# One decoder layer on one core: the attention's query and key stacks loaded with one DMA each, ahead of other loads

## The chip, the core and the metric

The kernel runs on one core of one Trainium2 chip. The core has five engines that each work through an instruction list of their own, in order: TensorE (PE in the profile, with its weight loads as PEld), VectorE (DVE), ScalarE (ACT), GpSimd (POOL) and SyncE (SP). Data moves between the memory of the chip and the on-chip memory of 128 partitions by DMA; here SP starts most transfers, ACT and POOL some, and the core's 16 DMA engines carry all of them. An instruction starts when the semaphores that it waits for have come and the one before it on its engine has left. The metric is the device time of one execution in microseconds (us), lower is better.

## The reference

The reference is one layer of a decoder over 1024 tokens of width 1024, in float32. Two kinds of attention run side by side and are merged by gates; a gated MLP with a causal convolution follows.

```python
xn = rmsnorm(x, norm_mix_w[l])
proj = xn @ w_in[l]
da_q, da_k, da_v, sw_q, sw_k, sw_v, g_da, g_sw = split_cols(proj)
y_da = diff_attention(da_q, da_k, da_v, lam, lam_init, subln_w[l])
y_sw = sliding_window_attention(sw_q, sw_k, sw_v, sinks[l])
merged = jax.nn.sigmoid(g_da) * (y_da @ w_br_da[l]) + jax.nn.sigmoid(g_sw) * (y_sw @ w_br_sw[l])
x = x + merged @ w_mix_out[l]
xn = rmsnorm(x, norm_ffn_w[l])
x = x + conv_ffn(xn, w_up[l], conv_w[l], conv_b[l], w_down[l])
```

The change touches the first kind, `diff_attention`, and the loads of the second. It has 4 heads with two query and key components of 64 each:

```python
s = jnp.einsum('bqhcd,bshcd->bhcqs', q_blk, k) * scale
logits = s - slopes[:, None, None, None] * dist.astype(jnp.float32)
logits = jnp.where(dist >= 0, logits, NEG_INF)
p = jax.nn.softmax(logits, axis=-1)
a = p[:, :, 0] - lam * p[:, :, 1]
return jnp.einsum('bhqs,bshe->bqhe', a.astype(v.dtype), v)
```

## The kernel before

**Two parts of a number.** TensorE multiplies numbers of reduced precision here, so the kernel keeps a value as a high part and a low part (what is left after rounding) and adds products of the parts. Queries and keys are stored that way in a buffer `qd` in the chip's memory: `qd[m, 0]` holds the high parts of the 128 channels of row block m, `qd[m, 1]` the low parts, each as 128 x 1024 (channel, token).

**The projection** makes query, key, value and gate channels in pairs of 128-row blocks; each pair is put together from seven partial products. The results stand in tiles `us`. `keep` stores queries and keys as high and low part (`qd<-hi` L628, `qd<-us` L629); gate blocks of these pairs are stored to `gd` at L589. The last of the pairs, blocks 21 and 22, are gates.

**The attention** starts at about 235 us. Its order is written out by hand in the table `STEPS`, whose words are run one after the other; a helper `in_order` keeps the engines to that order. The words that matter here are:
- `lqu_c` and `lku_c`: load of a query stack, and of two key stacks, for unit u and component c. A stack is a tile `u` of 128 partitions x 1024 tokens with 64 channels in its upper and 64 in its lower half. The query stack has the high parts in one half and the low parts in the other; the two key stacks repeat the high, and the low, parts in both halves. Product over 128 partitions of such stacks then sums high and low terms in one pass. There are 11 places for `u` tiles, handed out in turn (`turns`, `done`), and 36 stacks in all.
- `lvu`: load of a value block of unit u, into a tile `f` (`v32`, L796); `Xvu_0` and `Xvu_4`: its transposes on TensorE (L776).
- `Su_i_c`: scores of query block i (`sc<-u,u`, L811 for units 0 to 3; L953 for the sliding window, units 4 and 5), which read one query stack and two key stacks. `R` adds `bias` on VectorE (L817), `E` is the exponential on ScalarE (L822), `J` joins the two components.
- `Gm_h_p`: four products of gate blocks 23 to 33 (L295 to L297), set between the attention's steps, so that TensorE has work while VectorE and ScalarE are at the softmax. `wl`, `wc`, `wo` load their weights (`raw`, L264) and split them.

**Loads of a stack.** Each stack takes two DMAs of 64 partitions from SP, one a half:

```python
for part, to in enumerate((a, b)):
    self.nc.sync.dma_start(s[to].bitcast(F32), self.qd[m, part, a])
```

All of them, the weights' loads and the stores above stand in SP's one list. The bias table (128 x 1280) is loaded at L656 as the attention's tiles are set up. Where a tile lies is decided when it is first asked for, so that a stack can lie where a tile of the projection lay, and its load then waits until that tile has been read.

Of the kernel before, what the change touches and what calls it, by code (L numbers as in the profile page):

```python
# [17 lines left out]
P = 128  # L18
D = 1024
T = 1024  # L20
# [5 lines left out]
EPS = 1e-6  # L26
RAW = 3
GATE = 23
LATE = (21, 22, *range(26, 34))
HP, HPB, HR = 7, 13, 11  # L30
STORE = (1, 6)
# [13 lines left out]

STEPS = (
    """
    G23_0_0 G23_1_0 G23_0_1 G23_0_2 G23_0_3 Z0_0_0 G23_1_1 G23_1_2 g23_0 wl24 d23_0 wl25 wl26 G23_1_3 lv0 lv1 wc24 wo24 Xv0_0 wc25 wo25 g23_1 G24_0_0
    Z0_0_1 Z0_1_0 G24_0_1 Xv0_4 lq0_0 lq0_1 lk0_0 Hv0_4 Hv0_0 Wv0_0 Wv0_4 G24_0_2 G24_0_3 S0_0_0 G24_1_0 lk0_1 S0_1_0 g24_0 R0_0_0 S0_0_1 E0_0_0 R0_0_1
    E0_0_1 R0_1_0 E0_1_0 G24_1_1 S0_1_1 S0_2_0 J0_0 G24_1_2 lq1_0 R0_1_1 E0_1_1 X0_0_0 H0_0_0 S0_2_1 R0_2_0 S0_3_0 E0_2_0 J0_1 X0_1_0 wl27 H0_1_0 R0_2_1  # L50
    R0_3_0 lq1_1 G25_0_0 Z0_1_1 Z0_2_0 S0_3_1 W0_0_0 W0_1_0 A0_0 R0_3_1 Z0_2_1 lk1_0 E0_3_0 E0_2_1 J0_2 S0_4_0 G25_0_1 E0_3_1 K0_0 X0_2_0 J0_3 R0_4_0
    S0_4_1 d23_1 R0_4_1 H0_2_0 E0_4_0 X0_3_0 wl28 S0_5_0 G25_0_2 lv2 S0_5_1 W0_2_0 R0_5_0 S0_6_0 H0_3_0 W0_3_0 A0_1 E0_4_1 R0_5_1 E0_5_1 K0_1 G24_1_3 J0_4
    R0_6_0 Z0_3_0 X0_4_0 E0_5_0 X0_4_4 J0_5 H0_4_0 W0_4_0 S0_6_1 S0_7_0 G25_0_3 R0_6_1 H0_4_4 X0_5_0 W0_4_4 X0_5_4 d24_0 E0_6_0 H0_5_0 H0_5_4 S0_7_1 g24_1
    G25_1_0 lk1_1 R0_7_0 S1_0_0 W0_5_0 W0_5_4 A0_2 E0_6_1 E0_7_0 R0_7_1 sq0_0 E0_7_1 S1_0_1 J0_6 R1_0_0 X0_6_0 d24_1 G25_1_1 lq2_0 lq2_1 K0_2 X0_6_4 J0_7
    lk2_0 Z0_3_1 Z1_0_0 G25_1_2 H0_6_0 W0_6_0 X0_7_0 wc26 wo26 wl29 G25_1_3 H0_6_4 W0_6_4 X0_7_4 g25_0 H0_7_0 W0_7_0 E1_0_0 wc27 H0_7_4 S1_1_0 R1_0_1
    R1_1_0 E1_0_1 S1_1_1 R1_1_1 W0_7_4 A0_3 E1_1_1 cs0_0 E1_1_0 S1_2_0 S1_2_1 K0_3 sq0_1 wo27 Xv1_0 J1_0 cs0_1 R1_2_0 E1_2_0 ms0 G26_0_0 Xv1_4 J1_1 d25_0
    wl30 lv3 R1_2_1 Hv1_0 g25_1 Wv1_0 Hv1_4 Wv1_4 G26_0_1 E1_2_1 J1_2 d25_1 S1_3_0 S1_3_1 X1_0_0 Z1_0_1 R1_3_0 H1_0_0 X1_1_0 W1_0_0 H1_1_0 W1_1_0 G26_0_2
    S1_4_0 A1_0 pw0 sp0_0 R1_3_1 S1_4_1 R1_4_0 S1_5_0 ny0_0 X1_2_0 Z1_1_0 E1_3_0 E1_3_1 K1_0 sp0_1 J1_3 H1_2_0 R1_4_1 W1_2_0 G26_0_3 X1_3_0 H1_3_0 R1_5_0
    E1_4_0 ny0_1 E1_4_1 S1_5_1 Z1_1_1 W1_3_0 Z1_2_0 G26_1_0 R1_5_1 E1_5_1 A1_1 K1_1 S1_6_0 sq1_0 J1_4 R1_6_0 E1_5_0 E1_6_0 X1_4_0 Z1_2_1 X1_4_4 J1_5
    Z1_3_0 G26_1_1 H1_4_4 S1_6_1 S1_7_0 R1_6_1 H1_4_0 W1_4_0 G26_1_2 W1_4_4 E1_6_1 R1_7_0 X1_5_0 H1_5_0 W1_5_0 X1_5_4 H1_5_4 S1_7_1 S2_0_0 lk2_1 lq3_0  # L60
    R1_7_1 E1_7_0 E1_7_1 G26_1_3 wc28 W1_5_4 A1_2 K1_2 Z1_3_1 Z2_0_0 J1_6 R2_0_0 lq3_1 lk3_0 g26_0 X1_6_0 H1_6_0 S2_0_1 S2_1_0 X1_6_4 J1_7 H1_6_4 d26_0
    E2_0_0 G27_0_0 W1_6_0 W1_6_4 R2_0_1 E2_0_1 R2_1_0 X1_7_0 H1_7_0 W1_7_0 J2_0 X1_7_4 sy0 H1_7_4 W1_7_4 g26_1 G27_0_1 S2_1_1 S2_2_0 d26_1 A1_3 cs1_0
    Z2_1_1 R2_1_1 E2_1_0 R2_2_0 E2_1_1 E2_2_0 wo28 wl31 J2_1 S2_2_1 R2_2_1 K1_3 Xv2_0 S2_3_0 sq1_1 cs1_1 Hv2_0 Wv2_0 ms1 pw1 E2_2_1 J2_2 R2_3_0 G27_0_2
    Xv2_4 Hv2_4 S2_3_1 X2_0_0 E2_3_0 G27_1_0 Wv2_4 X2_1_0 H2_0_0 H2_1_0 Z2_0_1 Z2_1_0 S2_4_0 R2_3_1 E2_3_1 S2_4_1 W2_0_0 W2_1_0 A2_0 Z2_2_0 Z2_2_1 sp1_0
    R2_4_0 S2_5_0 Z2_3_0 J2_3 K2_0 ny1_0 E2_4_0 X2_2_0 H2_2_0 R2_4_1 E2_4_1 G27_0_3 lv4 sp1_1 W2_2_0 X2_3_0 H2_3_0 R2_5_0 E2_5_0 S2_5_1 S2_6_0 ny1_1
    G27_1_1 W2_3_0 R2_5_1 J2_4 R2_6_0 A2_1 E2_5_1 S2_6_1 K2_1 X2_4_0 E2_6_0 X2_4_4 J2_5 R2_6_1 H2_4_4 H2_4_0 W2_4_0 sq2_0 S2_7_0 G27_1_2 E2_6_1 X2_5_0
    H2_5_0 W2_4_4 X2_5_4 R2_7_0 H2_5_4 E2_7_0 S2_7_1 S3_0_0 W2_5_0 R2_7_1 E2_7_1 g27_0 G27_1_3 W2_5_4 A2_2 K2_2 lk3_1 lq4_0 lq4_1 J2_6 X2_6_0 R3_0_0
    S3_0_1 S3_1_0 lq4_2 X2_6_4 J2_7 Z2_3_1 Z3_0_0 H2_6_0 R3_0_1 G28_0_0 S3_1_1 R3_1_0 S3_2_0 d27_0 W2_6_0 H2_6_4 W2_6_4 E3_0_0 E3_0_1 J3_0 X2_7_0 X2_7_4
# [44 lines left out]
class Trunk:  # L113
# [281 lines left out]
    def project(self):  # L395
# [6 lines left out]
        with ExitStack() as ctx:  # L402
# [171 lines left out]
            for j, ms in enumerate(self.pairs):  # L574
                w = self.next_w()
                for _ in range(4):
                    with tc.issue_after(self.sync), tc.issue_after(self.sum):
                        next(sums, None)
                pp = {}
                for name, a, b in (prods[i] for i in ((0, 1, 4, 2, 3, 5, 6) if j == 0 else (0, 1, 2, 5, 3, 4, 6))):  # L580
                    pp[name] = bank()
                    self.product(pp[name], w[a], b)
                us = [self.tl(tp, [P, T], "us", bufs=3) for _ in range(2)]
                self.recombine(pp, us, tp, 0)
                for m, u in zip(ms, us):
                    if m < 21:
                        nc.gpsimd.tensor_tensor(u, u, self.rstd, ALU.mult)
                    if self.kind[m] == "g":
                        nc.sync.dma_start(self.gd[m - 18], u)  # L589
                    else:  # L590
                        self.keep(m, u, (tp, "hi"))
                if j == 5:
                    for n, t in enumerate(self.sum_pair((self.w_up[0], self.w_up[NF]))[2:]):
                        nc.sync.dma_start(self.su[n], t)
# [37 lines left out]
    def attention(self, gctx):  # L632
        nc, tc = self.nc, self.tc
        with ExitStack() as ctx:
            e = ctx.enter_context
            self.ap = e(tc.tile_pool(name="ap", bufs=1, side="right", reuse_waits="tile"))
            self.fpool = e(tc.tile_pool(name="fyp", bufs=1, side="right", reuse_waits="tile"))
            ap = self.ap

            lt = self.tl(self.gpool, [P, 64], "g0", bufs=1)  # L640
            ls = self.st.tile([P, 4], F32, name="ls")
            for c in range(2):
                a = C_LAM + 128 * c
                nc.vector.tensor_tensor(lt, self.vecs[:, a:a + 64], self.vecs[:, a + 64:a + 128], ALU.mult)
                nc.vector.tensor_reduce(ls[:, c:c + 1], lt, axis=mybir.AxisListType.X, op=ALU.add)
            nc.scalar.activation(ls[:, 2:4], ls[:, 0:2], AF.Exp)
            self.neglam = self.cp.tile([P, 1], F32, name="neglam")
            nc.vector.tensor_tensor(self.neglam, ls[:, 3:4], ls[:, 2:3], ALU.subtract)
            nc.vector.tensor_scalar(self.neglam, self.neglam, LAM_INIT, None, ALU.subtract)
            self.nsink = self.cp.tile([P, 8], F32, name="nsink")  # L650
            nc.vector.tensor_scalar(self.nsink, self.vecs[:, C_SINK:C_SINK + 8], -1.0, None, ALU.mult)
            self.subw = self.cp.tile([P, 1], F32, name="subw")
            nc.vector.tensor_scalar(self.subw, self.vecs[:, C_SUB:C_SUB + 1], 1.0 - LAM_INIT, None, ALU.mult)

            self.bias = ap.tile([P, T + 256], F32, name="bias")
            nc.sync.dma_start(self.bias, self.bias_d)  # L656

            self.step, self.free, self.held = {}, {}, {}
            self.actx = ctx.pop_all()
            for u in range(4):  # L660
                self.da_steps(u)
            for u in range(2):
                self.sw_steps(u)
            self.gate_steps()
            self.last_steps(gctx)
            self.last = {e: None for e in (self.hi.ins.engine, self.lo.ins.engine, self.pow.ins.engine, self.pe.engine)}
            with self.in_order(self.last):
                self.steps(0)
            assert not self.step, list(self.step)
# [23 lines left out]
    def gate_steps(self):  # L693
# [34 lines left out]
        for m in range(GATE, 34):  # L728
# [5 lines left out]
            for name, f in (("wl", load), ("wc", cast), ("wo", low)):  # L734
                at(f"{name}{m + 1}", f, m + 1)

    def stack_steps(self, u, qs, k, cs):

        v = {"q": [], "k": []}

        def q(m, c):
            a, b = slice(c * 64, c * 64 + 64), slice(64 - c * 64, 128 - c * 64)
            s = self.turns(self.ap, [P, T], "u", 11, F32R, uses=NB)
            for part, to in enumerate((a, b)):
                self.nc.sync.dma_start(s[to].bitcast(F32), self.qd[m, part, a])
            v["q"].append(s)

        def keys(c):
            r = []
            for part in range(2):  # L750
                t = self.turns(self.ap, [P, T], "u", 11, F32R, uses=NB)
                for to in range(2):
                    self.nc.sync.dma_start(t[64 * to:64 * to + 64].bitcast(F32), self.qd[k, part, c * 64:c * 64 + 64])
                r.append(t)
            v["k"].append(r)

# [32 lines left out]
    def da_steps(self, u):  # L789
# [3 lines left out]

        def v32():
            v["f"] = self.turns(self.fpool, [P, T], "f", 2, uses=2)
            nc.sync.dma_start(v["f"], self.qd[8 + u, 0])  # L796

        at(f"lv{u}", v32)
        value = lambda p: once(v, ("v", p), lambda: self.turns(ap, [P, NB, P], "v", 3, F32R, uses=4))
# [1140 lines left out]
```

## Time and profile before

| what | us |
|---|---|
| median of 3 runs | 1314.7 (1314.16 to 1314.91) |
| the profiled execution | 1317.12 |
| its span, first to last instruction | 1315.3 |
| DVE busy | 1062.6 |
| ACT busy | 667.2 |
| POOL busy | 457.7 |

The profile is one execution as the hardware's profiler recorded it. It has a page with totals, and a trace that answers finer questions. In a line of the timeline, the numbers are the start and the duration in us, then the engine, the line of the kernel, the operation, the tiles written and read (out<-in), how many instructions are merged in the row, and in brackets the idle time ahead of it with what ended it. SPq is SP as it starts DMAs; such a row tells when a transfer was issued, not when it landed. In a row of stretches, the columns are the stretch, its length, the busy time of each engine with the number of instructions, TensorE's granted clock as a share of full speed, the mean busy share of the 16 DMA engines, and what these moved in GB/s.

### The profile page before, as it was taken

The page shows a single profiled execution, that of the slowest core. Times are in us where ns is not written, and L with a number is a line of the kernel's source. Part 1 is how long each engine was busy: PE and PEld are TensorE (multiplying, and loading weights), DVE is VectorE, ACT ScalarE, POOL GpSimd, SP SyncE. Part 2 cuts the span into 40 slices and gives each one's busy share as a digit, 9 for nine tenths or more (in the row PEclk, how much of TensorE's full clock was granted, in tenths as well). Part 3 has the DMA queues.
Part 4 walks back from the last instruction along what each step waited for, and adds up shares of the span by engine and source line. Part 5 has one row for each costly group of instructions (what it writes and reads, how often), then busy time and mean ns, then how long its engine had stood idle before and what let it go on. Part 6 is the DMA issues. An engine that isn't in the chain of part 4 may idle for free. (4 is left out here: it accounts for less than half of the span.)

```text
span 1315.3 us, 17001 instructions
## 1 busy us (share of the span) xinstructions
PE 1298.1 (99%) x6162; PEld 1082.6 (82%) x6162; DVE 1062.6 (81%) x1416; ACT 667.2 (51%) x1065; POOL 457.7 (35%) x368
## 2 busy tenths in 40 slices
PE   9999999999999999999999999999999999999997
PEld 7888888788888888888777888888888888888886
DVE  8856775388989987976989988988898898896855
ACT  8422232166667776433655545454544544554543
POOL 0448675000001003210347667756676532000002
PEclk9999999999999999999999999999999999999999
DMA  7347786975555337335644456736554249733534
GB/s 295 114 173 178 218 242 197 253 200 132 151 133 136 135 92 281 128 124 172 210 136 158 164 148 149 209 125 150 185 140 124 71 142 333 290 100 119 158 96 148
DMA packets 79332, 220.63 MB, mean 168 GB/s; under 512 B 8849, under 2 KB 16657, under 8 KB 79121
## 3 DMA queue, kind: packets, MB, share of 16 engines
q1 hardware_dynamic: 64064, 190.71, 44.3%
q0 software_dynamic: 4608, 15.73, 7.4%
q10 hardware_dynamic: 10576, 13.11, 2.9%
q8 instruction: 48, 0.79, 0.2%
q14 instruction: 36, 0.29, 0.1%
HBM read 169.72 MB, written 81.26 MB: 191 GB/s over the span
## 5 line engine op out<-in xcount | busy, mean ns | idle before, releaser
L1683 POOL TENSOR_TENSOR us<-us,rstd 128x1024 f32<-128x1024 f32 x42 | 105.3, 2507 | 146.3 <-DVE us L1597 110.4
L225 DVE TENSOR_TENSOR sl<-sf,sh 128x1024 fp32r<-128x1024 f32 x44 | 108.2, 2462 | 2.3 <-ACT sh L218 2.3
L1609 DVE SCALAR_TENSOR_TENSOR c<-us,vecs,c 128x1024 f32<-128x1024 f32 x76 | 95.6, 1279 | 0.7
L1753 PE MATMUL y<-h,wh 128*128 128x512 f32 (+1 forms) x324 | 95.1, 377 | 0.0
L274 ACT CAST wh<-raw 128x768 fp32r<-128x768 f32 (+2 forms) x67 | 55.3, 827 | 75.9 <-PE y L1753 47.5
L276 DVE TENSOR_TENSOR wl<-raw,wh 128x768 fp32r<-128x768 f32 (+2 forms) x67 | 67.2, 1003 | 32.8 <-ACT wh L274 32.8
L312 POOL TENSOR_TENSOR rs<-ms,mhalf 128x2 f32<-128x2 f32 (+2 forms) x4 | 5.0, 1262 | 223.2 <-DVE ms L310 223.2
L1753 PE MATMUL d<-h,wh 128*128 128x512 f32 x264 | 81.3, 389 | 0.0
L295 PE MATMUL pg<-xh,wh 128*128 128x512 f32 x176 | 72.9, 414 | 0.0
L297 PE MATMUL pg<-xh,wl 128*128 128x512 f32 x176 | 69.6, 396 | 0.1
L296 PE MATMUL pg<-xl,wh 128*128 128x512 f32 x176 | 69.3, 394 | 0.0
L1753 PEld LDWEIGHTS y<-h,wh 128*128 128x128 f32 x324 | 59.4, 188 | 11.0
L1753 PE MATMUL y<-h,wl 128*128 128x512 f32 (+1 forms) x162 | 60.9, 376 | 0.0
L822 ACT ACTIVATE L<-L,sm 128x384 f32<-128x384 f32 (+7 forms) x64 | 49.6, 776 | 18.8 <-DVE sm L817 17.8
L1753 PEld LDWEIGHTS d<-h,wh 128*128 128x128 f32 x264 | 49.6, 188 | 10.3
L817 DVE CUSTOM_DVE_ANT_0 L<-sc,bias 128x128 f32<-128x128 f32 (+7 forms) x64 | 47.3, 752 | 11.8 <-PE sc L811 10.4
L780 ACT CAST aT<-t 128x512 fp32r<-128x512 f32 (+2 forms) x78 | 38.8, 521 | 28.9 <-PE t L776 26.4
L218 ACT CAST sh<-sf 128x1024 fp32r<-128x1024 f32 x44 | 46.3, 1053 | 10.2 <-POOL sf L204 6.1
L1753 PE MATMUL d<-h,wl 128*128 128x512 f32 x132 | 51.5, 390 | 0.0
L225 DVE TENSOR_TENSOR wl<-raw,wh 128x1024 fp32r<-128x1024 f32 (+1 forms) x23 | 27.5, 1200 | 28.9 <-ACT wh L218 28.9
L1193 POOL TENSOR_TENSOR rstd<-rstd,s 128x512 f32<-128x512 f32 x14 | 21.4, 1526 | 83.7 <-ACT s L1192 83.5
L833 POOL MEMSET aT<- 128x128 f32 x32 | 5.7, 207 | 127.3 <-PE t L843 86.6
(748 smaller groups left out, 4288.5 us busy)
## 6 DMA issues: line engine op xcount, KB each, us to landing
u<-qd SPq DMA_DIRECT2D x72, 256.0 KB, 6.7
raw<-in_w_up SPq DMA_DIRECT2D x24, 512.0 KB, 4.1
raw<-in_w_in SPq DMA_DIRECT2D x22, 512.0 KB, 4.7
rv<-in_w_up SPq DMA_DIRECT2D x22, 512.0 KB, 3.5
hd<-c SPq DMA_DIRECT2D x22, 512.0 KB, 4.5
sdP<-in_w_down POOLq DMA_DIRECT2D x16, 704.0 KB, 8.9
qd<-us SPq DMA_DIRECT2D x15, 512.0 KB, 3.5
raw<-sdP SPq DMA_DIRECT2D x16, 384.0 KB, 3.0
```

The costliest lines, as they stand in the source:

```text
L218: self.nc.scalar.copy(hi, src)
L225: self.nc.vector.tensor_tensor(lo, src, hi.bitcast(F32), ALU.subtract)
L274: self.hi = nc.scalar.copy(wh, raw)
L276: self.lo = (eng or nc.vector).tensor_tensor(wl, raw, wh.bitcast(F32), ALU.subtract)
L295: nc.tensor.matmul(ps, wh[:, kc + o, :], ah, start=first and n == 0, stop=False)
L296: nc.tensor.matmul(ps, wh[:, kc + o, :], al, start=False, stop=False)
L297: nc.tensor.matmul(ps, wl[:, kc + o, :], ah, start=False, stop=last and n == len(kcs) - 1)
L817: nc.vector.tensor_tensor_reduce(L[:, :w], v["sc", i, c][:, lo:lo + w], self.bias[:, o:o + w], slope, 3e38, ALU.add, ALU.min, small((i, c) ...
L822: nc.scalar.activation(L[:, :w], L[:, :w], AF.Exp, bias=s[:, 0:1], scale=-1.0, accum_out=s[:, 1:2] if c else s0()[:, i:i + 1])
L1609: nc.vector.scalar_tensor_tensor(c, us[:, 2 - n:T + 2 - n], cw[2 - n], c, ALU.mult, ALU.add)
L1683: i = (nc.vector if m % NF == 0 else nc.gpsimd).tensor_tensor(us[:, 2:], us[:, 2:], self.rstd, ALU.mult)
L1753: nc.tensor.matmul(ps, v[:, k - k0, :], x, start=start and k == i == 0, stop=k == HK - 1 and i == 2, skip_group_check=True)
```

## The change

Five edits go together.

1. A stack is loaded by one DMA of 128 partitions in place of two of 64. For a query stack the source is `qd[m, :, c*64:c*64+64]`, two blocks (high, low) of 64 rows of 1024. For a key stack it is one block of 64 rows, read twice by a broadcast to `[2, 64, T]`. A query stack has the high parts in its upper half for both components now.
2. In `STEPS`, the words `lq0_0 lk0_0 bias lq0_1 lk0_1 lv0` move to the head of the table, and `lv1` to a later place. The six stacks of unit 0, the bias and the value blocks of units 0 and 1 go through a new helper `first`, which gives the load a high priority and ties each to follow the one before it.
3. `PLACES` lists the attention's tiles; they are asked for in that order at once, which fixes where each lies.
4. The two gate stores of the last pair go from SP to POOL's queue.
5. The bias load is one of the words of the table, no longer at the setup.

```diff
+PLACES = "aT0 aT1 L0 L1 L2 L3 v0 u0 u1 u2 v1 aT2 aT3 u3 aT4 u6 u7 u4 u8 u9 u10 u5"
...
-    G23_0_0 G23_1_0 G23_0_1 G23_0_2 G23_0_3 Z0_0_0 G23_1_1 G23_1_2 g23_0 wl24 d23_0 wl25 wl26 G23_1_3 lv0 lv1 wc24 wo24 Xv0_0 wc25 wo25 g23_1 G24_0_0
+    lq0_0 lk0_0 bias lq0_1 lk0_1 lv0 G23_0_0 G23_1_0 G23_0_1 G23_0_2 G23_0_3 Z0_0_0 G23_1_1 G23_1_2 g23_0 wl24 d23_0 wl25 wl26 G23_1_3 wc24 wo24 Xv0_0
...
                     if self.kind[m] == "g":
-                        nc.sync.dma_start(self.gd[m - 18], u)
+                        (nc.gpsimd if j == len(self.pairs) - 1 else nc.sync).dma_start(self.gd[m - 18], u)
...
-            nc.sync.dma_start(self.bias, self.bias_d)
+            for n in PLACES.split():
+                self.tl(ap, [P, T], n, F32R if n[0] in "uva" else F32, bufs=1)
+            self.sp = None
...
+            self.at("bias", self.first, self.bias, self.bias_d)
...
+    def first(self, *a):
+        with self.tc.high_priority(600), self.tc.issue_after(self.sp) if self.sp is not None else nullcontext():
+            self.sp = self.nc.sync.dma_start(*a).ins
+
     def stack_steps(self, u, qs, k, cs):
 
         v = {"q": [], "k": []}
+        load = self.first if u == 0 else self.nc.sync.dma_start
 
         def q(m, c):
-            a, b = slice(c * 64, c * 64 + 64), slice(64 - c * 64, 128 - c * 64)
             s = self.turns(self.ap, [P, T], "u", 11, F32R, uses=NB)
-            for part, to in enumerate((a, b)):
-                self.nc.sync.dma_start(s[to].bitcast(F32), self.qd[m, part, a])
+            load(s.bitcast(F32), self.qd[m, :, c * 64:c * 64 + 64])
             v["q"].append(s)
 
         def keys(c):
             r = []
             for part in range(2):
                 t = self.turns(self.ap, [P, T], "u", 11, F32R, uses=NB)
-                for to in range(2):
-                    self.nc.sync.dma_start(t[64 * to:64 * to + 64].bitcast(F32), self.qd[k, part, c * 64:c * 64 + 64])
+                load(t.bitcast(F32), self.qd[k, part:part + 1, c * 64:c * 64 + 64].to_broadcast([2, 64, T]))
                 r.append(t)
...
-            nc.sync.dma_start(v["f"], self.qd[8 + u, 0])
+            (self.first if u < 2 else nc.sync.dma_start)(v["f"], self.qd[8 + u, 0])
```

The lists of TensorE, VectorE and ScalarE keep their instructions and their order; those of SP and POOL change. SP's list around the start of the attention, before, from the load of weights after which the stacks of the change will stand (`raw` are weights, `f` value blocks, `u` stacks; the row's number in the list comes first, and x2 is two DMAs in a row):

```order
78 L264 DMA raw_2006<-in_w_in 128x1024
79 L796 DMA f_304_2014<-qd 128x1024
80 L589 DMA gd<-us_1898 128x1024
81 L796 DMA f_305_2016<-qd 128x1024
82 L589 DMA gd<-us_1899 128x1024
83 L656 DMA bias<-in_bias 128x1280
84 L745 DMA u_316_2055<-qd 64x1024 x2
85 L745 DMA u_317_2058<-qd 64x1024 x2
86 L753 DMA u_318_2061<-qd 64x1024 x2
87 L753 DMA u_319_2064<-qd 64x1024 x2
88 L753 DMA u_324_2095<-qd 64x1024 x2
89 L753 DMA u_325_2098<-qd 64x1024 x2
```

And the same place of SP's list with the change, from the same load of weights:

```order
78 L265 DMA raw_2042<-in_w_in 128x1024
79 L743 DMA u_319_1974<-qd 128x1x1024
80 L743 DMA u_320_1976<-qd 128x1x1024
81 L743 DMA u_321_1978<-qd 128x1x1024
82 L743 DMA bias<-in_bias 128x1280
83 L743 DMA u_322_1981<-qd 128x1x1024
84 L743 DMA u_323_1983<-qd 128x1x1024
85 L743 DMA u_324_1985<-qd 128x1x1024
86 L743 DMA f_325_1987<-qd 128x1024
87 L743 DMA f_359_2157<-qd 128x1024
88 L752 DMA u_360_2159<-qd 128x1x1024
89 L265 DMA raw_2184<-in_w_in 128x1024
```

The six stacks stand ahead of the value blocks, the two gate stores have left the list, and the weights that stood seven stacks later (`raw_2169` before) now stand behind the six stacks and one of the next unit.

POOL's list with the change, at the end of the projection (`us` are its results, L588 scales them, `aT` are the attention's tiles, cleared by MEMSET):

```order
74 L588 TENSOR_TENSOR us_1779<-us_1779,rstd 128x1024
75 L588 TENSOR_TENSOR us_1780<-us_1780,rstd 128x1024
76 L590 DMA gd<-us_1898 128x1024
77 L590 DMA gd<-us_1899 128x1024
78 L839 MEMSET aT_328_2021 128x128
79 L839 MEMSET aT_340_2072 128x128
```

The two stores stand ahead of the first MEMSET of `aT`, which came straight behind the scaling before; the rest of the list is as it was.

More of the change, by code (lines that the diff above doesn't have):

```diff
@@ L47 @@
     """
-    G23_0_0 G23_1_0 G23_0_1 G23_0_2 G23_0_3 Z0_0_0 G23_1_1 G23_1_2 g23_0 wl24 d23_0 wl25 wl26 G23_1_3 lv0 lv1 wc24 wo24 Xv0_0 wc25 wo25 g23_1 G24_0_0
-    Z0_0_1 Z0_1_0 G24_0_1 Xv0_4 lq0_0 lq0_1 lk0_0 Hv0_4 Hv0_0 Wv0_0 Wv0_4 G24_0_2 G24_0_3 S0_0_0 G24_1_0 lk0_1 S0_1_0 g24_0 R0_0_0 S0_0_1 E0_0_0 R0_0_1
-    E0_0_1 R0_1_0 E0_1_0 G24_1_1 S0_1_1 S0_2_0 J0_0 G24_1_2 lq1_0 R0_1_1 E0_1_1 X0_0_0 H0_0_0 S0_2_1 R0_2_0 S0_3_0 E0_2_0 J0_1 X0_1_0 wl27 H0_1_0 R0_2_1
-    R0_3_0 lq1_1 G25_0_0 Z0_1_1 Z0_2_0 S0_3_1 W0_0_0 W0_1_0 A0_0 R0_3_1 Z0_2_1 lk1_0 E0_3_0 E0_2_1 J0_2 S0_4_0 G25_0_1 E0_3_1 K0_0 X0_2_0 J0_3 R0_4_0
@@ L52 @@
[L52 to L63, printed above, removed]
@@ L64 @@
-    Xv2_4 Hv2_4 S2_3_1 X2_0_0 E2_3_0 G27_1_0 Wv2_4 X2_1_0 H2_0_0 H2_1_0 Z2_0_1 Z2_1_0 S2_4_0 R2_3_1 E2_3_1 S2_4_1 W2_0_0 W2_1_0 A2_0 Z2_2_0 Z2_2_1 sp1_0
-    R2_4_0 S2_5_0 Z2_3_0 J2_3 K2_0 ny1_0 E2_4_0 X2_2_0 H2_2_0 R2_4_1 E2_4_1 G27_0_3 lv4 sp1_1 W2_2_0 X2_3_0 H2_3_0 R2_5_0 E2_5_0 S2_5_1 S2_6_0 ny1_1
+    lq0_0 lk0_0 bias lq0_1 lk0_1 lv0 G23_0_0 G23_1_0 G23_0_1 G23_0_2 G23_0_3 Z0_0_0 G23_1_1 G23_1_2 g23_0 wl24 d23_0 wl25 wl26 G23_1_3 wc24 wo24 Xv0_0
+    wc25 wo25 g23_1 G24_0_0 Z0_0_1 Z0_1_0 G24_0_1 Xv0_4 Hv0_4 Hv0_0 Wv0_0 Wv0_4 G24_0_2 G24_0_3 S0_0_0 G24_1_0 S0_1_0 g24_0 R0_0_0 S0_0_1 E0_0_0 R0_0_1
@@ new lines @@
+    E0_0_1 R0_1_0 E0_1_0 G24_1_1 S0_1_1 S0_2_0 J0_0 G24_1_2 lv1 lq1_0 R0_1_1 E0_1_1 X0_0_0 H0_0_0 S0_2_1 R0_2_0 S0_3_0 E0_2_0 J0_1 X0_1_0 wl27 H0_1_0
+    R0_2_1 R0_3_0 lq1_1 G25_0_0 Z0_1_1 Z0_2_0 S0_3_1 W0_0_0 W0_1_0 A0_0 R0_3_1 Z0_2_1 lk1_0 E0_3_0 E0_2_1 J0_2 S0_4_0 G25_0_1 E0_3_1 K0_0 X0_2_0 J0_3
+    R0_4_0 S0_4_1 d23_1 R0_4_1 H0_2_0 E0_4_0 X0_3_0 wl28 S0_5_0 G25_0_2 lv2 S0_5_1 W0_2_0 R0_5_0 S0_6_0 H0_3_0 W0_3_0 A0_1 E0_4_1 R0_5_1 E0_5_1 K0_1
+    G24_1_3 J0_4 R0_6_0 Z0_3_0 X0_4_0 E0_5_0 X0_4_4 J0_5 H0_4_0 W0_4_0 S0_6_1 S0_7_0 G25_0_3 R0_6_1 H0_4_4 X0_5_0 W0_4_4 X0_5_4 d24_0 E0_6_0 H0_5_0 H0_5_4
@@ new lines @@
+    S0_7_1 g24_1 G25_1_0 lk1_1 R0_7_0 S1_0_0 W0_5_0 W0_5_4 A0_2 E0_6_1 E0_7_0 R0_7_1 sq0_0 E0_7_1 S1_0_1 J0_6 R1_0_0 X0_6_0 d24_1 G25_1_1 lq2_0 lq2_1 K0_2
+    X0_6_4 J0_7 lk2_0 Z0_3_1 Z1_0_0 G25_1_2 H0_6_0 W0_6_0 X0_7_0 wc26 wo26 wl29 G25_1_3 H0_6_4 W0_6_4 X0_7_4 g25_0 H0_7_0 W0_7_0 E1_0_0 wc27 H0_7_4 S1_1_0
+    R1_0_1 R1_1_0 E1_0_1 S1_1_1 R1_1_1 W0_7_4 A0_3 E1_1_1 cs0_0 E1_1_0 S1_2_0 S1_2_1 K0_3 sq0_1 wo27 Xv1_0 J1_0 cs0_1 R1_2_0 E1_2_0 ms0 G26_0_0 Xv1_4 J1_1
+    d25_0 wl30 lv3 R1_2_1 Hv1_0 g25_1 Wv1_0 Hv1_4 Wv1_4 G26_0_1 E1_2_1 J1_2 d25_1 S1_3_0 S1_3_1 X1_0_0 Z1_0_1 R1_3_0 H1_0_0 X1_1_0 W1_0_0 H1_1_0 W1_1_0
@@ new lines @@
+    G26_0_2 S1_4_0 A1_0 pw0 sp0_0 R1_3_1 S1_4_1 R1_4_0 S1_5_0 ny0_0 X1_2_0 Z1_1_0 E1_3_0 E1_3_1 K1_0 sp0_1 J1_3 H1_2_0 R1_4_1 W1_2_0 G26_0_3 X1_3_0 H1_3_0
+    R1_5_0 E1_4_0 ny0_1 E1_4_1 S1_5_1 Z1_1_1 W1_3_0 Z1_2_0 G26_1_0 R1_5_1 E1_5_1 A1_1 K1_1 S1_6_0 sq1_0 J1_4 R1_6_0 E1_5_0 E1_6_0 X1_4_0 Z1_2_1 X1_4_4
+    J1_5 Z1_3_0 G26_1_1 H1_4_4 S1_6_1 S1_7_0 R1_6_1 H1_4_0 W1_4_0 G26_1_2 W1_4_4 E1_6_1 R1_7_0 X1_5_0 H1_5_0 W1_5_0 X1_5_4 H1_5_4 S1_7_1 S2_0_0 lk2_1
+    lq3_0 R1_7_1 E1_7_0 E1_7_1 G26_1_3 wc28 W1_5_4 A1_2 K1_2 Z1_3_1 Z2_0_0 J1_6 R2_0_0 lq3_1 lk3_0 g26_0 X1_6_0 H1_6_0 S2_0_1 S2_1_0 X1_6_4 J1_7 H1_6_4
@@ new lines @@
+    d26_0 E2_0_0 G27_0_0 W1_6_0 W1_6_4 R2_0_1 E2_0_1 R2_1_0 X1_7_0 H1_7_0 W1_7_0 J2_0 X1_7_4 sy0 H1_7_4 W1_7_4 g26_1 G27_0_1 S2_1_1 S2_2_0 d26_1 A1_3
+    cs1_0 Z2_1_1 R2_1_1 E2_1_0 R2_2_0 E2_1_1 E2_2_0 wo28 wl31 J2_1 S2_2_1 R2_2_1 K1_3 Xv2_0 S2_3_0 sq1_1 cs1_1 Hv2_0 Wv2_0 ms1 pw1 E2_2_1 J2_2 R2_3_0
+    G27_0_2 Xv2_4 Hv2_4 S2_3_1 X2_0_0 E2_3_0 G27_1_0 Wv2_4 X2_1_0 H2_0_0 H2_1_0 Z2_0_1 Z2_1_0 S2_4_0 R2_3_1 E2_3_1 S2_4_1 W2_0_0 W2_1_0 A2_0 Z2_2_0 Z2_2_1
+    sp1_0 R2_4_0 S2_5_0 Z2_3_0 J2_3 K2_0 ny1_0 E2_4_0 X2_2_0 H2_2_0 R2_4_1 E2_4_1 G27_0_3 lv4 sp1_1 W2_2_0 X2_3_0 H2_3_0 R2_5_0 E2_5_0 S2_5_1 S2_6_0 ny1_1
```

## The prediction

> **What bounds the kernel now.** I read the page first, for the engine that sets the time, then TensorE's waits, then the timeline where those waits lie, and last what the DMA engines moved there.
>
> ```profile
> span 1315.3 us, 17001 instructions
> PE 1298.1 (99%) x6162; PEld 1082.6 (82%) x6162; DVE 1062.6 (81%) x1416; ACT 667.2 (51%) x1065; POOL 457.7 (35%) x368
> u<-qd SPq DMA_DIRECT2D x72, 256.0 KB, 6.7
> ```
>
> TensorE is busy for 1298.1 of 1315.3 us, so the kernel is TensorE's list, whose order and instructions the change leaves alone. Only 17.2 us of idle time, and slow stretches, could be won. To lose time is easier: whatever makes TensorE wait adds to the end one for one. The third line gives what is changed: 72 half stacks of 256 KB, 6.7 us from issue to landing in the median. The waits of TensorE that hang on these loads:
>
> ```profile
> engine line waited for: us in total, times, longest us
> PE sc L811 <- DMA u<-qd: 2.6, 2, 1.8
> ...
> PE sc L953 <- DMA u<-qd: 1.4, 1, 1.4
> ...
> PE sc L811 <- issue: 0.3, 1, 0.3
> ```
>
> The timeline of TensorE shows where they fall:
>
> ```profile
> 246.79 0.60 PE L776 MATMUL t<-ident,f 128*128 128x128 f32 x4
> ...
> 254.28 0.36 PE L811 MATMUL sc<-u,u 128*128 128x256 f32 x1 [0.81 <-DMA u<-qd]
> ...
> 258.69 0.55 PE L811 MATMUL sc<-u,u 128*128 128x256 f32 x1 [1.78 <-DMA u<-qd]
> 259.04 0.63 PE L295 MATMUL pg<-xh,wh 128*128 128x512 f32 x1
> ...
> 261.60 0.88 PE L811 MATMUL sc<-u,u 128*128 128x256 f32 x4
> 262.32 0.40 PE L295 MATMUL pg<-xh,wh 128*128 128x512 f32 x1
> 262.56 0.39 PE L296 MATMUL pg<-xl,wh 128*128 128x512 f32 x1
> ```
>
> The first scores wait for their stacks, twice; after the second wait six products take 2.56 us (259.04 to 261.60), at 0.43 us each, where at 262.32 the same product gives way after 0.24. That is 6 x 0.19 = 1.1 us more, a slowed clock. SP's timeline tells why the stacks are late:
>
> ```profile
> 229.51 0.33 SPq L264 DMA_DIRECT2D raw<-in_w_in  x1
> 233.15 0.32 SPq L796 DMA_DIRECT2D f<-qd  x1
> ...
> 237.19 0.49 SPq L656 DMA_DIRECT2D bias<-in_bias  x1
> 241.56 2.40 SPq L745 DMA_DIRECT2D u<-qd  x4
> 244.01 8.07 SPq L753 DMA_DIRECT2D u<-qd  x8
> ```
>
> Their first issue comes at 241.56, behind the last gate store (SP waited 3.8 us for it), and the half loads then land one after the other. SP's own wait, and the stretches with what the DMA engines moved:
>
> ```profile
> SPq L745 <- DMA gd<-us: 3.8, 1, 3.8
> ```
>
> ```profile
> 10.00:15.00 5.00, 4.06 (x19) 3.05 (x18) 4.73 (x7) 4.89 (x7) 0.00 (x0) 1.00 1.04 419
> 252.00:262.00 10.00, 7.12 (x27) 5.45 (x27) 3.46 (x12) 1.48 (x6) 0.00 (x0) 0.83 1.04 247
> 229.00:432.00 203.00, 198.74 (x1204) 174.39 (x1203) 165.21 (x425) 119.99 (x294) 15.03 (x53) 0.99 0.63 169
> ```
>
> With the 16 engines full (share 1.04) they move 419 GB/s of loads over 128 partitions, 26.2 GB/s an engine, but only 247 GB/s, 15.4 an engine, where half stacks of 64 partitions run. So the shape of a transfer sets how well the engines carry it, at the same share of busy time.
>
> **The change, part by part.** All sums are made on the profiled execution (1317.1 us; span 1315.3); the median of the runs is 2.4 us below it, which I take off at the end.
>
> *What the early issue could win.* If the stacks were there in time, the waits of 2.6, 0.3 and 1.4 us and the slowed 1.1 us would go: 5.4 us. The rest of TensorE's idle time has other releasers and stays. This is the ceiling of the gain.
>
> *The gate stores on POOL, the bias, the places.* POOL issues the two stores just ahead of a MEMSET of `aT`, where it stands idle:
>
> ```profile
> 236.85 0.21 POOL L833 MEMSET aT<- 128x128 f32 x1 [10.64 <-DVE us L611]
> 241.61 0.50 POOL L833 MEMSET aT<- 128x128 f32 x3 [4.55 <-issue]
> L167 POOL DMA_DIRECT2D sm<-in_w_mix x16: 811/1070/1448, 109.2 to 213.9; - x16
> L1075 SPq DMA_DIRECT2D ga<-gd x3: 319/374/424, 489.4 to 533.5; - x3
> ```
>
> Issuing a transfer holds POOL for 1.07 us (the third row's median), two stores some 2.1 us, inside the 4.55 us for which POOL stands still anyway; the first reader of gate data of any kind comes at 489.4. If that cover were gone, 2.1 us would be the price. I cost it at nothing. The bias moves ahead of its old issue at 237.19, still before the scores. The new places let the first stack go out behind the weights of 229.51, some 12 us sooner than 241.56: its place no longer lies on a projection tile that is still being stored.
>
> *The stack as one DMA.* This is the term that decides. The destination is 128 partitions, but the source of each of the 36 loads is written as two blocks of 64 rows, and for keys as the same block read twice. No other transfer of the program has a first dimension of two, so no row shows its price; it lies between the nearest rows. At the least the 16 engines share the load as they share a load over 128 partitions: 524 KB at 419 GB/s is 1.25 us. At the most only the two blocks are dealt out, one to an engine: two engines at 15.4 GB/s take 17.0 us, and at 26.2 GB/s 10.0 us. Bandwidth that follows the shape of the pattern is what the two stretches above show; what is dealt out must then be sought in the pattern, and its first dimension now counts two. I therefore take two engines, at 26.2 GB/s, since two engines have none of the crowding of 16: **10.0 us a stack**, against 2 x 1.06 = 2.1 us before (262 KB at 247 GB/s, twice). The full spread stays as a rival.
>
> The Trainium skill ("DMA: Bandwidth & Descriptors", section "Why a DMA increments its semaphore by 16 and not by 1") says that the hardware looks at the slowest dimension over 1 of each side and uses the largest number of engines, up to 16, that divides both; its table of best practices warns of a leading broadcast of c copies, which leaves at most c engines. By this, 2 and 128 give two engines, and the sum is the one below; the same page's advice for one transfer over 128 partitions in place of two over disjoint halves would give the rival's. No transfer of before can show it.
>
> *The sum.* In the first group, the value block `f` stands behind six stacks and the bias. From an issue at 229.9 and data from some 231: 6 x 10.0, then the bias (655 KB) and `f` (524 KB), spread over 16 engines, 1.6 + 1.25 us, and some 1 us to land: about 295. Its transposes stand in TensorE's list at 246.79. All that TensorE has behind them waits: **some 48 us** at the first stop. From there the stacks themselves go on setting the pace. All 36 must have come when the last unit's scores start:
>
> ```profile
> 432.14 1.12 PE L953 MATMUL sc<-u,u 128*128 128x256 f32 x8
> ```
>
> Their transfers take 36 x 10.0 = 360 us on the two engines. The other traffic has its share there too: 169 GB/s for 203 us is 34.3 MB, less 72 x 0.262 = 18.9 MB of stacks is 15.4 MB; a sixteenth of it at 26.2 GB/s is 37 us for each engine. So the last stack lands at about 231 + 360 + 37 + 1 = 629 in place of being there by 432.14, and all that follows moves by **197 us**. With 11 places for stacks, loads are issued ahead of use, so that the two engines have little reason to stand idle; where a place is given back late, the sum grows. The waits won above are inside this chain and add nothing. From 1317.1 + 197 = 1514, less 2.4, comes 1512; I say 1510.
>
> **Rivals.** *Full spread, faster.* All 16 engines carry a stack in 1.25 us. Six stacks, bias and `f` then take 7.5 + 1.6 + 1.25 us from 231, and with 1 us to land they are there by 243, before 246.79. All 5.4 us are won: 1314.7 - 5.4 = 1309.3. Up to 2.0 us a stack (6 x 2.0 + 2.85 + 1 from 231) `f` is there by 246.79, and that is the point from which it decides. For it speaks that the destination is 128 partitions like that of the 419 GB/s row; against it, the two blocks of the source.
>
> *Full spread, but at the rate of the half stacks.* At 15.4 GB/s an engine a stack takes 2.1 us; six, with the bias (2.7) and `f` (2.1), come to 17.5 us, and `f` lands at about 249.5, 2.7 us late for 246.79, while the stacks' own waits vanish. 1314.7 - 5.4 + 2.7 = 1312.0, at the border of what can be told from no change. For it speaks that the rows read from `qd` are the same 4 KB rows; against it, that the slow rate was seen with 64 partitions alone.
>
> *Two engines at the slow rate.* 17.0 us a stack: 231 + 612 + 37 + 1 = 881, a delay of 449 us, about 1764. The slow rate came with 16 engines working at once on 64 partitions; two do not crowd like that, so this is far less likely.
>
> **How the numbers follow.** Two engines at about 10 us a stack: 0.82, at the slow rate: 0.03; full spread: 0.11; full spread at the slow rate: 0.04. The predicted time is the first case's. Its own range: 9 us a stack and half of the other traffic gives 231 + 324 + 18 + 1 = 574, 142 us late, about 1457; 12 us a stack (half way to the slow rate is 13.5) gives 231 + 432 + 37 + 1 = 701, 269 late, about 1584. I set 1440 to 1600, for gaps on either side; with nearly all of the 0.82 inside it holds 8 times in 10. The tail below is the full spread. A measurement of this kernel can tell about 0.2% from no change, 2.6 us. Faster by more: the full spread and none other, 0.11; within: 0.04; slower: 0.85.
>
> **What would show it.** Two engines: the median from issue to landing of `u<-qd` (36 of 512 KB) rises from 6.7 us to some tens of us, as loads of 10 us stand in line; the DMA share over the attention falls to about 2/16 = 0.13 for the stacks plus 15.4 MB of the rest, some 0.2, and the rate below 100 GB/s; TensorE's idle time rises to about 200 us, nearly all ended by `DMA u<-qd`, `f<-qd` and weights behind them; the first stop lies at the transposes of `f`, some 48 us long; after the attention nothing differs. Full spread: six stacks landed by 243, no wait of L811 for `u<-qd`, no products at 0.63 us. What would make it wrong: a first dimension of two that is merged with the second on the way to the engines, which the landing of the very first stack tells: after 3 us or after 11 and more.

## The result and the profile after

| | before | with the change |
|---|---|---|
| median, us | 1314.7 (1314.16 to 1317.01, 5 runs) | 1519.2 (1518.61 to 1521.72, 5 runs) |
| ratio to before | | 1.155, 95% interval 1.154 to 1.157 |
| span of the profiled execution | 1315.3 | 1516.8 |
| mean granted clock of TensorE | 0.997 | 0.932 |

The changed kernel takes 204.5 us more, 15.5%. The head of its page, the row of the stacks' loads (to which the page gives no time to landing), and TensorE's waits, in us in total, times, longest:

```profile
span 1516.8 us, 16948 instructions
...
PE 1315.6 (87%) x6162; PEld 1095.3 (72%) x6162; DVE 1063.6 (70%) x1416; ACT 666.9 (44%) x1065; POOL 459.2 (30%) x370
...
u<-qd SPq DMA_DIRECT2D x36, 512.0 KB
```

```profile
PE sc L817 <- DMA u<-qd: 83.0, 8, 23.5
PE t L782 <- DMA f<-qd: 54.4, 1, 54.4
PE sc L959 <- DMA u<-qd: 22.2, 2, 20.6
PE t L985 <- DVE aT L789: 11.0, 1, 11.0
PE sc L959 <- issue: 8.8, 1, 8.8
PE sc L817 <- issue: 8.4, 1, 8.4
```

TensorE's instructions are as many as before, 6162; its idle time went from 17.2 to 1516.8 - 1315.6 = 201.2 us. Loads from `qd` end 159.6 us of it (83.0 + 54.4 + 22.2). The 17.5 us by which its busy time grew go with the clock: in the first two us after the first stop the granted clock is 0.50, and a product takes 0.63 us there in place of 0.39.

What the DMA engines did, in stretches of the same columns as before: one within the first stop, and one over the attention up to the last stack:

```profile
256.00:285.00 29.00, 0.00 (x0) 0.00 (x0) 0.00 (x0) 0.00 (x0) 0.00 (x0) 0.50 0.13 53
229.00:633.00 404.00, 216.06 (x1203) 186.96 (x1201) 166.76 (x425) 121.37 (x297) 16.23 (x56) 0.75 0.23 85
```

In the first, no engine computes at all, TensorE waits, work stands in SP's queue, and yet the DMA engines are busy for 0.13 of their time: 2.1 of 16. They move 53 GB/s, 26 GB/s for each of two. This one line points at the cause; what makes it two is for the experiments to show.

When a stack landed can be read from the updates of the semaphores in the trace: the first at 245.8, 16 us after its issue, the second at 257.1, and so on to the last at 633.2, one every 11.1 us in the mean. The first value block landed at 301.0, just behind the sixth stack (299.7). The timelines of SP and TensorE show the first stop and the last one:

```profile
229.86 12.20 SPq L743 DMA_DIRECT2D u<-qd  x3
242.10 10.37 SPq L743 DMA_DIRECT2D bias<-in_bias  x1
252.58 22.74 SPq L743 DMA_DIRECT2D u<-qd  x3
275.42 10.75 SPq L743 DMA_DIRECT2D f<-qd  x2
```

```profile
301.00 1.12 PE L782 MATMUL t<-ident,f 128*128 128x128 f32 x4 [54.36 <-DMA f<-qd]
...
631.36 0.28 PE L959 MATMUL sc<-u,u 128*128 128x256 f32 x1
633.28 0.98 PE L959 MATMUL sc<-u,u 128*128 128x256 f32 x6 [1.65 <-DMA u<-qd]
```

The transposes that stood at 246.79 start at 301.00; the scores that stood at 432.14 run at 631.36 and, after a last wait, 633.28: 201 us late, which is the whole difference of the spans (201.5). Nothing after the attention adds or wins.

### The profile page after: what moved, and what is told of

Read it like the earlier page. It is cut to its first block, busy times and chain, and to the rows that moved or that the text cites. A ratio compares the mean times of both kernels' runs of the same rounds, so it can differ in the third digit from the quotient of the medians.

```text
span 1516.8 us, 16948 instructions
## 1 busy us (share of the span) xinstructions
PE 1315.6 (87%) x6162; PEld 1095.3 (72%) x6162; DVE 1063.6 (70%) x1416; ACT 666.9 (44%) x1065; POOL 459.2 (30%) x370
## 5 line engine op out<-in xcount | busy, mean ns | idle before, releaser
L817 PE MATMUL sc<-u,u 128*128 128x512 f32 (+2 forms) x192 | 46.7, 366 | 91.3 <-DMA u<-qd 83.0
L789 DVE TENSOR_TENSOR aT<-t,aT 128x512 fp32r<-128x512 f32 (+2 forms) x78 | 45.7, 604 | 83.5 <-ACT aT L786 83.2
L817 PEld LDWEIGHTS sc<-u,u 128*128 128x128 f32 x192 | 32.3, 196 | 96.7 <-DMA u<-qd 77.3
L1759 PEld LDWEIGHTS y<-h,wh 128*128 128x128 f32 x324 | 59.4, 188 | 11.1
L782 PE MATMUL t<-ident,f 128*128 128x128 f32 x32 | 5.4, 295 | 54.4 <-DMA f<-qd 54.4
```

Of the source, the lines that this page charges most:

```text
L817: nc.tensor.matmul(sc[:, lo + n0:lo + n1], v["q"][c][:, i * P:(i + 1) * P], v["k"][c][part][:, n0:n1], start=part == 0, stop=part == 1)
L1759: nc.tensor.matmul(ps, v[:, k - k0, :], x, start=start and k == i == 0, stop=k == HK - 1 and i == 2, skip_group_check=True)
```

## The experiments

Three theories were set against one another. Theory 1: the first dimension of the access pattern sets how many DMA engines carry a transfer, so a first dimension of two leaves two. Theory 2: the merged load is slow for another reason, the two sources of a query stack or the zero step of a key stack's broadcast. Theory 3: the loss comes from the other edits, the early place of the loads in SP's list and the new places in memory.

| run | loads of stacks | rest | time, us | ratio to before |
|---|---|---|---|---|
| e1_halves | 2 x 64 partitions | changed | 1321.4 | 1.0044 (1.0031 to 1.0057) |
| e2_rows | one, rows first | changed | 1313.5 | 0.9988 (0.9979 to 0.9997) |
| e3_q_two | queries two first, keys rows first | changed | 1384.4 | one run |
| e4_first_dim_4 | 2 x 64 partitions, 4 first | changed | 1365.9 | one run |
| e5_halves_dim_2 | 2 x 64 partitions, 2 first | changed | 1523.9 | one run |
| e6_halves_dim_8 | 2 x 64 partitions, 8 first | changed | 1337.3 | one run |
| e7_before_two | one, two first | before | 1523.2 | one run |
| e8_before_rows | one, rows first | before | 1311.2 | 0.9962 (0.9949 to 0.9976) |
| e9_rows_again | as e2_rows | changed | 1312.9 | 0.9980 (0.9971 to 0.9989) |
| e10_before_rows_again | as e8_before_rows | before | 1310.4 | 0.9964 (0.9950 to 0.9978) |

**Halves again.**

```diff
-            load(s.bitcast(F32), self.qd[m, :, c * 64:c * 64 + 64])
+            for part in range(2):
+                load(s[64 * part:64 * part + 64].bitcast(F32), self.qd[m, part, c * 64:c * 64 + 64])
...
-                load(t.bitcast(F32), self.qd[k, part:part + 1, c * 64:c * 64 + 64].to_broadcast([2, 64, T]))
+                for to in range(2):
+                    load(t[64 * to:64 * to + 64].bitcast(F32), self.qd[k, part, c * 64:c * 64 + 64])
```

> The changed kernel, but each stack again by two DMAs of 64 partitions (high parts in the upper half for both components). If the first dimension of two is the cause (theory 1), all of the loss of 204.5 us goes, and what is left is the early issue: 1309 us (1306 to 1314), with the waits of L811 for stacks gone. If the early places of the loads or the tiles' new places are the cause (theory 3), it stays near 1519. If one DMA over two sources is slow in itself (theory 2), it comes back too, so this run tells theory 3 from the others only.

Measured: 1321.4 us. All but 6 us of the loss is gone, which rules theory 3 out as its main cause. But the gain that was expected of the early issue isn't there either: the kernel is 0.44% slower than before. The trace shows the new wait of TensorE, a wait of SP, and what the DMA engines did as that one ended:

```profile
254.85 1.12 PE L784 MATMUL t<-ident,f 128*128 128x128 f32 x4 [8.07 <-DMA f<-qd]
```

```profile
SPq L743 <- DMA gd<-g: 9.5, 1, 9.5
```

```profile
247.00:248.00 1.00, 0.00 (x0) 0.00 (x0) 0.28 (x1) 0.69 (x1) 0.00 (x0) 1.00 0.00 0
```

A half load of the fifth stack waited 9.5 us for a gate store that ScalarE had issued. The two have no data in common: the DMAs of SP and ScalarE share eight completion semaphores, and this load was given the one that the store still held. The value block stood behind it and was late by 8.1 us. The shared semaphore explains only some 2 us of that, though. By the semaphores' updates the half loads ahead were still landing until 247.2, and the DMA engines stood empty from there to about 248.8. The larger part is the order itself: before, the value block was issued ahead of all stacks; here it comes behind twelve half loads, which land 1.1 us apart, and the bias. With one DMA a stack (the next run) it was a load of weights that met such a wait, of 11.0 us.

**One load, rows first.** The remedy for the pattern: the 64 rows become the first dimension, the two blocks the second.

```diff
-            load(s.bitcast(F32), self.qd[m, :, c * 64:c * 64 + 64])
+            load(s.bitcast(F32), self.qd[m, :, c * 64:c * 64 + 64].rearrange("h r t -> r h t"))
...
-                load(t.bitcast(F32), self.qd[k, part:part + 1, c * 64:c * 64 + 64].to_broadcast([2, 64, T]))
+                load(t.bitcast(F32), self.qd[k, part:part + 1, c * 64:c * 64 + 64].to_broadcast([2, 64, T]).rearrange("h r t -> r h t"))
```

> The changed kernel with one DMA a stack, its source read with the 64 rows as first dimension and the two blocks (or the two copies) as second, so that partition 2r and 2r+1 hold row r of the one and the other; queries and keys are laid out alike, so the products sum the same terms. Theory 1: 16 engines carry each load, 1.25 us a stack, 1309 us (1305 to 1313). Theory 2 (a source of two blocks, or the zero step of the broadcast, is slow in itself): 10 us a stack as before, about 1519.

Measured: 1313.5 us, the profiled span 1310.2. The same bytes, the same 36 DMAs, the same zero step, the same place in SP's list, and 206 us less. Theory 2 falls. The gain on before is smaller in the medians (1.7 us) than in the profile (5.1 us). SP's timeline, against that of the changed kernel above:

```profile
230.24 1.90 SPq L743 DMA_DIRECT2D u<-qd  x3
232.18 0.77 SPq L743 DMA_DIRECT2D bias<-in_bias  x1
233.05 2.01 SPq L743 DMA_DIRECT2D u<-qd  x3
235.80 1.81 SPq L743 DMA_DIRECT2D f<-qd  x2
```

Six stacks, the bias and two value blocks are issued within 8 us; there it took 56.

**Two first for the query stacks alone.** Queries take the loads of the change, keys those with rows first. The two lay out their channels in different ways then, so the scores of this run are not the reference's; the work is the same.

> As the run with rows first, but the 16 query stacks keep the two blocks as first dimension; the 20 key stacks have rows first. Theory 1: 16 x 10.0 + 20 x 1.25 + 37 us of the rest is 222 us, the last stack there at 454 in place of 432: some 22 us over the kernel before, about 1335 (1320 to 1350). If only the zero step of the key loads is slow: about 1310.

Measured: 1384.4 us, 69 over before, where 22 were forecast. The zero step is not needed for a loss: 16 loads without one do a third of it. The size is a miss, outside its range, and its kind is told below.

**Four, two and eight as first dimension**, with two DMAs of 64 partitions a stack and no broadcast. The diff is against the run with halves, for 4; the others put 2 and 8.

```diff
-                load(s[64 * part:64 * part + 64].bitcast(F32), self.qd[m, part, c * 64:c * 64 + 64])
+                load(s[64 * part:64 * part + 64].bitcast(F32), self.qd[m, part, c * 64:c * 64 + 64].rearrange("(r g) t -> g r t", g=4))
```

> As the run with halves, but each half's 64 rows are read as 4 x 16 (row 4r+g as row r of group g; the same for queries and keys, so the products sum the same terms). Nothing else differs: two DMAs of 64 partitions a stack. Theory 1: four engines, 262 KB in 2.5 us, 5.0 us a stack: the value block of the first group at 231 + 30 + 4 = 265 in place of 246.8, the last stack at 231 + 180 + 37 + 1 = 449 in place of 432: 15 to 35 us over the kernel before, about 1337. Theory 2: like the run with halves, about 1309.

> As the run with halves (two DMAs of 64 partitions a stack), but each half's 64 rows are read as 2 x 32 (row 2r+g as row r of group g; the same for queries and keys). One block of memory, no broadcast, 64 partitions: all that is left of the change's form is the first dimension of two. Theory 1: 262 KB on two engines, 5.0 us a half, 10.0 us a stack: back to the changed kernel's time, 1519 us (1500 to 1545). Theory 2 (merged loads or the zero step): like the run with halves, 1321.

> The same with 8 x 8. Theory 1: eight engines at 26.2 GB/s take 1.25 us a half, 2.5 us a stack against some 2.2 us with 64 rows as first dimension: 2 us more at the first stop than in the run with halves, and little later: 1324 us (1319 to 1335). If the loss comes from a first dimension under 16 as such, and not from the number of engines: about 1360, as with four.

Measured: 1523.9, 1365.9 and 1337.3 us for 2, 4 and 8, beside 1321.4 for 64. With two, a load of one block, of 64 partitions, without any broadcast, gives the changed kernel's time: the first dimension of the source alone is enough, and nothing else of the form is needed. The excess over the run with halves, 202.6, 44.5 and 15.9 us, falls with the number, so there is no border at 16 below which all are alike. The times with 4 and 8 lie above their forecasts (1337 and 1324) and outside the ranges that went with them (15 to 35 us over before, and up to 1335). Stretches from the first stacks in the runs with eight, with four and with two, chosen where hardly any other transfer runs:

```profile
241.00:244.00 3.00, 3.00 (x15) 2.49 (x14) 0.69 (x1) 0.10 (x1) 0.00 (x0) 1.00 0.51 210
```

```profile
247.00:258.00 11.00, 0.77 (x4) 0.31 (x2) 2.03 (x3) 1.04 (x1) 0.00 (x0) 0.71 0.26 105
```

```profile
265.00:285.00 20.00, 0.00 (x0) 0.00 (x0) 0.00 (x0) 0.00 (x0) 0.00 (x0) 0.50 0.13 53
```

The shares times 16 are 8.2, 4.2 and 2.1 engines, and the rates are 26 GB/s for each of 8, 4 and 2: so many engines carry a load as its first dimension counts.

**The loads of the change in the kernel before**, two first, then rows first.

```diff
-            for part, to in enumerate((a, b)):
-                self.nc.sync.dma_start(s[to].bitcast(F32), self.qd[m, part, a])
+            self.nc.sync.dma_start(s.bitcast(F32), self.qd[m, :, c * 64:c * 64 + 64])
...
-                for to in range(2):
-                    self.nc.sync.dma_start(t[64 * to:64 * to + 64].bitcast(F32), self.qd[k, part, c * 64:c * 64 + 64])
+                self.nc.sync.dma_start(t.bitcast(F32), self.qd[k, part:part + 1, c * 64:c * 64 + 64].to_broadcast([2, 64, T]))
```

> The kernel before with the change's loads of stacks alone: one DMA a stack, first dimension two; order, places, gate stores and bias as before. Theory 1: the stacks go out from 241.6, 36 x 10.0 + 37 us of the rest on the two engines, the last there at 243 + 397 + 1 = 641 in place of 432: 209 us late, about 1524 (1500 to 1545), so that this edit alone does all of the loss. If the early places have a share in it: clearly less.

> The kernel before with one DMA a stack and rows as first dimension; order, places, gate stores and bias as before. Six stacks from 241.6 at some 1.6 us each are there by about 253, when the second component's scores are due at 258: the waits of L811 (2.6 and 0.3 us) and the slowed products (1.1 us) go, without the early issue: 1311 us (1309 to 1314), the same within 2 us as the changed kernel with rows first. If the early issue is what wins: no better than before, 1315.

Measured: 1523.2 and 1311.2 us. Of the change's five edits the first does all of the loss. And the same edit with rows first is the gain that the change could have had: 0.38% faster than before, with SP's order left as it was. TensorE's one wait for a stack in that run, and the DMA engines where before they moved 247 GB/s:

```profile
PE sc L950 <- DMA u<-qd: 0.3, 1, 0.3
```

```profile
252.00:262.00 10.00, 10.00 (x52) 8.43 (x51) 7.07 (x25) 4.55 (x16) 0.00 (x0) 1.00 1.02 417
```

Of the 4.0 us of waits for stacks 0.3 are left, the clock in this stretch is 1.00, and the same engines, as busy as before, carry 417 GB/s.

**Both with rows first, on one chip.**

> The changed kernel with rows as first dimension, beside the next run on the same chip. If the early issue, the places and the stores on POOL are worth nothing once a stack lands in 1.2 us: the same as the next run within 1 us, both about 4 us under the kernel before. If they cost something (the value block now behind six stacks, 0.4 us of wait seen): 1 to 2 us slower than the next run, as the two medians on different chips say.

> The kernel before with rows as first dimension and nothing else of the change, beside the run above: 0.9960 of the kernel before (0.994 to 0.998).

Measured: 1312.9 against 1310.4 us, ratios to before 0.9980 and 0.9964, whose intervals overlap a little. The early issue, the places and the stores on POOL win nothing once a stack lands in time; that they cost some 2 us is likely by both pairs of runs, but which of them does was not tried. The fastest version is the kernel before with rows first, 0.36% (0.22 to 0.50) under before in this repeat.

## Why the prediction was right

- **The term that decides, 10.0 us a stack.** Right. In the first stop two engines' worth is busy and moves 53 GB/s, 9.9 us a stack. That it is the first dimension was chosen in the prediction, not seen; the runs with 2, 4, 8 and 64 show it now. The reason given for the fast rate holds too: two engines load 64 partitions at 26 GB/s each in the run with halves and two first, and the slow 15.4 was seen only with 16 engines at once. The rule of the Trainium skill ("DMA: Bandwidth & Descriptors", "Why a DMA increments its semaphore by 16 and not by 1") gives two engines for this pattern, and four and eight for the others; the shares of 0.13, 0.26 and 0.51 agree with it.
- **The sum, 197 us.** Right: 201. The last stack was put at 629, and it landed at 633.2. One stack landed every 11.1 us, where the sum has 10.0 and 37/36 us of the rest. The rest is as large as forecast, since 85 GB/s for 404 us are 34.3 MB as before. And the two engines did hardly pause, as the sum supposes: up to the last landing fewer than two packets were under way for 2 us in all.
- **The first stop, 48 us.** It lasted 54.4. The prediction counted only the bias and the value block beside the six stacks. On the two engines there also ran their shares of the weights issued just ahead, of the two gate stores on POOL and of one gate store of ScalarE: 1.8 MB, of which a sixteenth takes 4.4 us at 26.2 GB/s. That is most of the 6 us; the rest is open. The prediction did not see that SP would be held: the third stack's issue held it until 242, the bias's until 252, and the value block went out after 275. This cost the value block little, as its share on the two engines stood behind the sixth stack anyhow, and the sum did not suffer.
- **The gate stores, the bias and the places at nothing.** About right against a loss of 200 us: with rows first the whole rest of the change loses some 2 us (1312.9 against 1310.4). A gate store held POOL for 0.64 and 0.55 us, not 1.07.
- **The ceiling of 5.4 us.** Right in its mechanism and size for the loads: with rows first in the kernel before, the profiled span falls by 5.7 us (3.9 of idle time, 1.8 of busy time), the medians by 4.7 and 5.3. It needed one DMA over 128 partitions on 16 engines, not the early issue.
- **The rivals.** The full spread was not wrong as a mechanism, it only belongs to another pattern. The slow rate of 15.4 GB/s an engine on two engines did not occur.
- **The signs.** DMA share 0.23 where some 0.2 was given, 85 GB/s where less than 100, idle time 201 where about 200, nothing after the attention. The median time to landing, from the semaphores' updates, is 34 us, and the first stack landed after 16. Less right is that nearly all idle time would be ended by these loads: 159.6 of 201.2 us are, and some 28 are put down to VectorE or to nothing that the profile shows.
- **Where the same sum failed.** In the experiments, for 16 stacks on two engines (69 us, forecast 22) and for four and eight engines (51 and 21 us over before, forecast 22 and 9). The sum takes the transfers as back to back, which holds only while the engines are saturated: 36 stacks on two. Below that, stops come one by one, at the first value block and at each unit's first scores, and in between the engines have idle time that the sum doesn't count: with four, fewer than four packets were under way for 22 of the 249 us up to the last landing, with eight fewer than eight for 53 of 220. In the run with four, the first stop alone was 26.7 us, where 18 were forecast. How much of the idle time is SP's held issue, and how much loads that wait for a place, was not taken apart.

## What to carry to other kernels

Look at the first dimension of a DMA's source, not only at its partitions and bytes: one transfer over 128 partitions whose source starts with a dimension of two ran at about a fifth of the speed of the two transfers that it replaced (53 against 247 GB/s), and with the same dimensions in the other order at 1.7 times their speed. Where a sum over channels follows, the order of the channels over the partitions is free, so the larger dimension can be put first at no cost. In a stretch in which only such transfers run, the mean DMA share times 16 is the number of DMA engines at work, and a share of 0.13 with TensorE waiting is read at once. An early issue is paid for by the loads that it is put ahead of: the value block came 8.1 us late behind twelve half loads, and 0.4 us behind six whole ones.

## What the runs showed of the hardware

- A transfer that runs on few DMA engines also holds the engine that issues it: the first two stacks took SP 0.6 us each to issue, the third 10.9, and of the next six issues four took 9.7 to 12.4 us, about a stack's own transfer time. SP's list then stands still, and weights and bias that could go to idle engines wait behind. With rows first SP issued three stacks in 1.9 us.
- A load that is spread over all 16 engines also waits for the two that are busy: the value block landed 1.2 us after the sixth stack.
- The trace tells the number of engines a second way: packets of 4 bytes. They are 16 to every DMA before (8721 = 545 x 16 + 1), and 2 to a stack with the change (7641 = 473 x 16 + 36 x 2 + 1); by the same count 4 and 8 to a half load with a first dimension of four and eight.
- Half loads over 64 partitions keep 16 engines busy (share 1.04) at 247 GB/s, and the same rows loaded over 128 partitions (1.02) at 417, some other loads among both.
- A wait of SP between two transfers with nothing in common, 9.5 us, came from a shared completion semaphore alone; some 2 us of it reached the DMA engines.
